# A two-layer encoder trunk on one core: attention outputs from halves, neighbourhood scores over 40 of 64 grid columns, squares on ScalarE, roots put off

## The chip, the cores and the metric

The kernel runs on one core of one Trainium2 chip. The metric is device time in microseconds. Five engines work side by side, each through its own instructions in order: TensorE (PE; its weight loads are listed apart, as PEld), VectorE (DVE), ScalarE (ACT), GpSimd (POOL) and SyncE (SP), which issues all the DMAs here. A change of time within about 0.2% can't be told from none.

## What is computed

Two layers over 256 tokens of 2048 features, float32. Each layer modulates its norms by six vectors made from `c`, runs two attentions side by side with a sigmoid gate each, and then a gated MLP with a convolution over three positions.

```python
for l in range(DEPTH):
    mod = c_act @ ada_w[l] + ada_b[l]
    h = rmsnorm(x, norm_mix[l]) * (1.0 + sc_a) + sh_a
    qa, ka, va, qb, kb, vb, ga, gb = split_cols(h @ w_in[l])
    # A: 8 heads, 2 groups of k and v, q and k normed by head, partial rotary
    ya = window_attention(qa, ka, va, sink_a[l]) @ w_proj_a[l]
    # B: 8 heads, q and k normed by head; tokens lie on a grid of 4 rows of 64 columns
    yb = neighbourhood_attention(qb, kb, vb, rel_bias_b[l]) @ w_proj_b[l]
    merged = jax.nn.sigmoid(ga) * ya + jax.nn.sigmoid(gb) * yb
    x = x + gt_a * (merged @ w_out[l])
    h = rmsnorm(x, norm_ffn[l]) * (1.0 + sc_m) + sh_m
    u = depthwise_conv(h @ w_up[l], conv_w[l], conv_b[l])
    g, v = jnp.split(u, 2, axis=-1)
    x = x + gt_m * ((jax.nn.silu(g) * v) @ w_down[l])
```

In attention A a token sees all tokens up to 128 away. In B it sees all four grid rows, but of each only the 16 columns of a window around its own column, held inside the grid: tokens of columns 0 to 31 see none beyond column 39, and those of 32 to 63 none before 24.

## The kernel before

**The weight stream.** All weights pass once, in units of 16 blocks of 128 x 128 (1 MB). `unit` (L246) loads a unit by one DMA into `raw` (four buffers, shared with the rows `aw` of the modulation weights), and splits each half of it into `hl` (four buffers): the high half is a cast to float32r on ACT (L260), the low half the difference, on DVE (L261). A product of float32 accuracy is then three float32r matmuls: high by high, high by low, low by high (L269 to L271 for a feature block, 256 columns each; L327 to L329 for a token block, 512 columns).

**Ticks.** After each unit `Stream.tick` calls `bg.tick()` and `plan`. `bg` holds deferred functions, called at the next tick, and jobs with a rate, steps per tick. `plan` pulls rows of the modulation (`aw`, L191 and L192, a DMA of 1 MB and a DVE instruction over 2048 elements) by a table of units, ADA_PLAN. So program order is set by ticks; within it the framework's scheduler orders each engine's instructions.

**One layer.** Nine groups of q, k and v columns (in layer 0 four passes over parts of the 16 chunks, with partial sums added into `packs` at L762; in layer 1 one pass, straight out of PSUM), gate A, proj_a over the eight outputs `oA` of attention A, gate B, the merge over `oB`, the output projection, and the MLP. After a group of q or k, `qk_rows` (L487) squares it (L494), sums by head (L495), takes the power −0.5 on POOL (L389), and defers `norm` (L500: DVE multiplies, rotary), which defers `turn` (L523: PE transposes `qtp`, ACT writes q or k transposed with its gain). `turn` then counts the group as ready.

**Attention** is a job: heads are launched once their group is ready, one a step, and each live head goes on by one step: bias load (B only), then `attend` (L535): scores `sc` on PE in float32, masked maximum on DVE (L543), exponential with its sum on ACT (L551), scaling (L559); then transposes `tp` (L564) and a copy (L566); then the product `po` with v in float32 (L570), and its halves (L572, L573). Rates are ATT (1.288 steps a tick in layer 0, 0.4 in layer 1) and, from gate B on, ATT_B (0.21). Before proj_a, `attended(HA)` steps the job until all A heads are done; `bg.finish(job)` before the merge does the rest.

**Bare.** At a layer's start and in the MLP's first chunks, matmuls run on x before the norm's scale is known (class `Bare`, L428): a bare chunk has 256 columns and two more for the shift, a high and a low part in each of its two halves, and `level` (L479) scales the result afterwards. All three matmuls of a block have 258 columns there.

Of the kernel before, what the change touches and what calls it, by code (L numbers as in the profile page):

```python
# [15 lines left out]
P = 128  # L16
# [13 lines left out]
GRID_W, NA_KH, NA_KW = 64, 8, 16  # L30

# [32 lines left out]
ATT = [1.288, 0.4]  # L64
ATT_B = [0.21, 0.21]
# [50 lines left out]
def encoder(ctx: ExitStack, tc: tile.TileContext, a: dict, out: bass.AP):  # L116
# [33 lines left out]
    one = sm.tile([1, P], F32, name="one", tag="one", bufs=1)  # L150
    nc.vector.memset(one[:], 1.0)
    for i in range(0, D, 512):
        cb = ax.tile([P, 512], F32, name="cb", tag="ax")
        nc.tensor.matmul(cb[:], one[:], cact[:1, i : i + 512], start=True, stop=True)
# [3 lines left out]
    skip(224)  # L158
# [106 lines left out]
    def feature_block(ps, hl, j, act, first, last):  # L265

        hi, lo = hl[:, 0, j * P : (j + 1) * P], hl[:, 1, j * P : (j + 1) * P]
        out = ps[:, : act.shape[-1]]
        nc.tensor.matmul(out, hi, act[:, 0], start=first, stop=False)  # L269
        nc.tensor.matmul(out, hi, act[:, 1], start=False, stop=False)  # L270
        nc.tensor.matmul(out, lo, act[:, 0], start=False, stop=last)  # L271
# [72 lines left out]

    def half_tanh(dst, src, **kw):

        nc.scalar.activation(out=dst, in_=src, func=AF.Tanh, scale=0.5, **kw)
# [12 lines left out]
    class Squares:  # L360
# [6 lines left out]
        def add(self, mo):  # L367
            sq = self.acc if mo == 0 else ev.tile([P, S], F32, name="sq", tag="r")
# [59 lines left out]
    class Bare:  # L428
# [23 lines left out]
        def add(self, kc):  # L452
            need(self.l, 48 * self.w + 2 * kc + 2)
            c, scale = self.chunks[kc], amods[self.l][:, self.w, kc : kc + 1]
            sh = mods[self.l][:, 3 * self.w * KC + kc : 3 * self.w * KC + kc + 1]
            nc.scalar.activation(out=c[:, 0, :S], in_=x[:, kc], func=AF.Identity, scale=scale)
            nc.vector.scalar_tensor_tensor(
                out=c[:, 1, :S], in0=x[:, kc], scalar=scale, in1=c[:, 0, :S].bitcast(F32), op0=ALU.mult, op1=ALU.subtract
            )
            sh = sh.broadcast_to([P, 2])  # L460
            nc.scalar.copy(c[:, 0, S:], sh)
            nc.vector.tensor_tensor(out=c[:, 1, S:], in0=sh, in1=c[:, 0, S:].bitcast(F32), op=ALU.subtract)
# [24 lines left out]
    def qk_rows(pss, heads, rot, gain, dst, then):  # L487

        cols = 0
        n = heads * HEAD  # L490
        ss = sm.tile([P, 8], F32, name="qss", tag="qss")
        for t, ps in enumerate(pss):
            sq = at.tile([P, 512], F32, name="qsq", tag="qsq", bufs=1)
            nc.scalar.activation(out=sq[:, :n], in_=ps[:, cols : cols + n], func=AF.Square)  # L494
            nc.vector.tensor_reduce(  # L495
                out=ss[:, t * heads : (t + 1) * heads], in_=sq[:, :n].rearrange("p (h d) -> p h d", d=HEAD), axis=AX.X, op=ALU.add
            )
        rs = sm.tile([P, 8], F32, name="qrs", tag="qrs")
        rsqrt(rs[:, : 2 * heads], ss[:, : 2 * heads], HEAD, 2 * heads)
        def norm():  # L500
            qn = at.tile([P, 2, 4, HEAD], F32, name="qn", tag="qn", bufs=1)
            for t, ps in enumerate(pss):
                nc.vector.tensor_tensor(  # L503
                    out=qn[:, t, :heads],
                    in0=ps[:, cols : cols + n].rearrange("p (h d) -> p h d", d=HEAD),
                    in1=rs[:, t * heads : (t + 1) * heads].unsqueeze(2).broadcast_to([P, heads, HEAD]),
                    op=ALU.mult,
                )
# [14 lines left out]
        def turn(qn):  # L523
            for t in range(2):
                ps = ax.tile([P, 4, P], F32, name="qtp", tag="ax")
                for h in range(heads):
                    nc.tensor.transpose(ps[:, h], qn[:, t, h], ident[:])
                nc.scalar.activation(
                    out=dst[:, :, t * P : (t + 1) * P], in_=ps[:, :heads], func=AF.Identity, scale=gain
                )  # L530
            then()

        bg.defer(norm)

    def attend(qT, kT, v, mask, scale, sink, o):  # L535

        sc = ax.tile([P, 2, S], F32, name="sc", tag="ax")
        for t in range(2):
            nc.tensor.matmul(sc[:, t], qT[:, t * P : (t + 1) * P], kT, start=True, stop=True)  # L539
        p = at.tile([P, 2, S], F32, name="p", tag="p")  # L540
        m = sm.tile([P, 2], F32, name="m", tag="m")
        for t in range(2):
            nc.vector.tensor_tensor_reduce(  # L543
                out=p[:, t], in0=sc[:, t], in1=mask[:, t], scale=scale, scalar=-3.0e38 if sink is None else sink,
                op0=ALU.add, op1=ALU.max, accum_out=m[:, t : t + 1],
            )
# [3 lines left out]
        for t in range(2):  # L550
            nc.scalar.activation(out=p[:, t], in_=p[:, t], func=AF.Exp, bias=nm[:, t : t + 1], accum_out=den[:, t : t + 1])  # L551
# [6 lines left out]
        for t in range(2):  # L558
            nc.scalar.activation(out=p[:, t], in_=p[:, t], func=AF.Copy, scale=ri[:, t : t + 1])  # L559
# [5 lines left out]
        pT = at.tile([P, 2, S], F32, name="pT", tag="pT", bufs=1)  # L565
        nc.scalar.copy(pT[:], tp[:])  # L566
        yield
        po = ax.tile([P, 512], F32, name="po", tag="ax")
        for k in range(2):
            nc.tensor.matmul(po[:, :S], v(k), pT[:, k], start=k == 0, stop=k == 1)  # L570
        o = o()
        nc.scalar.copy(o[:, 0], po[:, :S])  # L572
        nc.vector.tensor_tensor(out=o[:, 1], in0=po[:, :S], in1=o[:, 0].bitcast(F32), op=ALU.subtract)  # L573
# [60 lines left out]
    def small(l):  # L634
# [5 lines left out]
        rg = load(a["rg"][l], [P, 2, ROT], f"rg{l}", lay, tag="rg")  # L640
# [4 lines left out]
        for w in range(2):  # L645
            rot = lay.tile([P, 4, 2, HALF], F32, name=f"rot{l}_{w}", tag=f"rot{w}")
# [9 lines left out]
    for l in range(L):  # L656
# [31 lines left out]
        def va(k, g):  # L688
            return packs[0][:, 2 * k + 1, g * HEAD : (g + 1) * HEAD]
# [4 lines left out]
        def head_a(i):  # L694
# [3 lines left out]
            elif i % 2 == 0:  # L698
# [4 lines left out]
                qTa[:, i], kTa[:, g], lambda k: va(k, g), tables[0], SCALE, sink[:, i : i + 1], lambda: oA[i],  # L703
            )

        def head_b(hb):
# [3 lines left out]
            nc.sync.dma_start(bias[:], a["bias"][l, hb])  # L710
            yield
            yield from attend(
                b[:, 8 + i], b[:, i], lambda k: v[:, k, i * HEAD : (i + 1) * HEAD], bias, 1.0, None,
                lambda: oB_of(hb),
# [31 lines left out]
        for pi, part in enumerate(parts):  # L746
# [4 lines left out]
            for g in range(len(QKV_GROUPS)):  # L751
# [26 lines left out]
                elif vcol is None:  # L778
                    qk_rows(pss, 4, None, gains[:, 3:4] if g in (3, 6) else gains[:, 2:3], dst, have)
# [21 lines left out]
        attended(HA)  # L801
        for mo in range(KC):
# [219 lines left out]
```

## Time and profile before

| | before |
|---|---|
| median of 3 runs | 2705.58 us |
| lowest and highest | 2704.58, 2707.64 us |
| span of the profiled execution | 2703.4 us |
| scores, mean of a record | 382 ns (A), 380 ns (B) |
| output products, mean of a record | 386 ns (A), 391 ns (B) |
| bare matmuls, mean | 284 to 288 ns |
| stream matmuls of 256 columns, mean | 277 to 278 ns |

The profile is of an execution of its own; its span is what all places in time refer to, from 0 to 2703.4. A float32 matmul leaves two records. Matmuls are pipelined, so a record is longer than the step from one start to the next; the steps are read off the timeline. In a group's row stand busy time, mean of one, idle time of the engine before it, and what ended that.

### The profile page before, as it was taken

Reading aid. Unit: us, or ns where it says so; the run is one execution under the profiler, and the core shown is the slowest. Engines: PE = TensorE matmul, PEld = TensorE weight load, DVE = VectorE, ACT = ScalarE, POOL = GpSimd, SP = SyncE. Lnnn points to the kernel's source line nnn. Section 1 sums busy time; section 2 is a strip of 40 time slices with the busy share of each in tenths; the row PEclk is TensorE's granted clock in tenths of the full one; section 3 lists DMA queues with packets and bytes.
Section 4 is the critical chain, followed back from the end, with each engine's and each line's share of the span. In section 5 each row is a group of like instructions: output and inputs, shape, how many; then the busy total and the mean of one; then the engine's idle time right before and its main releaser. Section 6 shows DMA issues by size and latency. Waiting matters only on the chain.

```text
span 2703.4 us, 50143 instructions
## 1 busy us (share of the span) xinstructions
PE 2661.1 (98%) x21088; PEld 2566.7 (95%) x21088; DVE 2099.6 (78%) x2941; ACT 1375.9 (51%) x2026; POOL 34.2 (1%) x24
## 2 busy tenths in 40 slices
PE   7899999999999999999999999999999999999999
PEld 5788799999999999999998889999999999999999
DVE  6998988897988888788886666658879866665664
ACT  5344674455753555355554555544565445544553
POOL 0000100000000000000000000000000000000000
PEclk9999999999999999999999999999999999999999
DMA  8887578986678877887756656666757775555554
GB/s 319 335 335 269 218 282 333 355 316 257 224 291 320 298 272 281 315 295 278 294 211 253 243 203 238 226 244 249 293 183 284 284 257 201 188 197 193 189 199 144
DMA packets 101892, 700.38 MB, mean 259 GB/s; under 512 B 12705, under 2 KB 15009, under 8 KB 17697
## 3 DMA queue, kind: packets, MB, share of 16 engines
q1 hardware_dynamic: 101666, 697.17, 70.3%
q8 instruction: 165, 2.70, 0.4%
q14 instruction: 61, 0.50, 0.0%
HBM read 695.03 MB, written 2.10 MB: 258 GB/s over the span
## 4 chain that ended last, share of the span: by engine, by line
PE 88%; DVE 6%; DMA 2%; issue 2%; ACT 1%; POOL 1%; SPq 0%; DVEq 0%; POOLq 0%; ACTq 0%
PE ps L269 24%; PE ps L271 24%; PE ps L270 24%; PE ps_t L328 4%; PE ps_t L329 4%; PE ps_t L327 4%; DMA aw<-in_aw 2%; DVE hl L261 2%; DVE aw L192 2%; PE po L570 1%; PE sc L539 1%; POOL qrs L389 1%; PE tp L564 0%; ACT hl L260 0%; DVE qn L503 0%
## 5 line engine op out<-in xcount | busy, mean ns | idle before, releaser
L261 DVE TENSOR_TENSOR hl<-w,hl 128x1024 fp32r<-128x1024 f32 x928 | 1129.7, 1223 | 342.1 <-ACT hl L260 341.1
L260 ACT CAST hl<-w 128x1024 fp32r<-128x1024 f32 x928 | 970.6, 1049 | 786.4 <-PE ps L271 497.1
L269 PE MATMUL ps<-h,hl 128*128 128x256 f32 x3328 | 925.7, 278 | 0.0
L271 PE MATMUL ps<-h,hl 128*128 128x256 f32 x3328 | 923.1, 277 | 0.0
L270 PE MATMUL ps<-h,hl 128*128 128x256 f32 x3328 | 922.6, 277 | 0.0
L269 PEld LDWEIGHTS ps<-h,hl 128*128 128x128 f32 x3328 | 625.9, 188 | 0.6
L270 PEld LDWEIGHTS ps<-h,hl 128*128 128x128 f32 x3328 | 625.3, 188 | 0.6
L271 PEld LDWEIGHTS ps<-h,hl 128*128 128x128 f32 x3328 | 625.4, 188 | 0.2
L192 DVE CUSTOM_DVE_ANT_0 aw<-aw,cact,ab 128x2048 f32<-128x2048 f32 x192 | 450.8, 2348 | 73.3 <-DMA aw<-in_aw 72.8
L327 PE MATMUL ps_t<-hl,h 128*128 128x512 f32 x576 | 226.4, 398 | 8.0 <-ACT hl L260 7.3
L328 PE MATMUL ps_t<-hl,h 128*128 128x512 f32 x576 | 227.4, 395 | 5.2 <-DVE hl L261 5.2
L329 PE MATMUL ps_t<-hl,h 128*128 128x512 f32 x576 | 227.0, 394 | 0.9 <-DVE h L418 0.9
L867 DVE SCALAR_TENSOR_TENSOR u<-ps,cw,u 128x255 f32<-128x255 f32 x304 | 146.4, 481 | 89.0 <-ACT u L865 84.5
L865 ACT ACTIVATE u<-ps,cw 128x256 f32<-128x256 f32 x152 | 85.6, 563 | 202.5 <-PE ps L271 202.5
L271 PE MATMUL ps<-merged,hl 128*128 128x256 f32 x512 | 142.1, 278 | 0.4 <-DVE hl L261 0.4
L270 PE MATMUL ps<-merged,hl 128*128 128x256 f32 x512 | 141.7, 277 | 0.0
L269 PE MATMUL ps<-merged,hl 128*128 128x256 f32 x512 | 141.7, 277 | 0.0
L271 PE MATMUL ps<-act_o,hl 128*128 128x256 f32 x512 | 141.5, 276 | 0.0
L270 PE MATMUL ps<-act_o,hl 128*128 128x256 f32 x512 | 141.5, 276 | 0.0
L269 PE MATMUL ps<-act_o,hl 128*128 128x256 f32 x512 | 141.2, 276 | 0.0
L327 PEld LDWEIGHTS ps_t<-hl,h 128*128 128x128 f32 x576 | 109.1, 190 | 31.8 <-ACT hl L260 8.4
L328 PEld LDWEIGHTS ps_t<-hl,h 128*128 128x128 f32 x576 | 109.0, 189 | 30.6 <-DVE hl L261 8.2
(205 smaller groups left out, 4543.2 us busy)
## 6 DMA issues: line engine op xcount, KB each, us to landing
w<-in_ws SPq DMA_DIRECT2D x464, 1024.0 KB, 4.9
aw<-in_aw SPq DMA_DIRECT2D x192, 1024.0 KB, 4.9
bias<-in_bias SPq DMA_DIRECT2D x16, 256.0 KB, 5.0
x<-in_xT SPq DMA_DIRECT2D x4, 512.0 KB, 5.4
out<-x SPq DMA_DIRECT2D x16, 128.0 KB, 2.0
cw<-in_cw SPq DMA_DIRECT2D x2, 176.0 KB, 3.3
maskA<-in_maskA SPq DMA_DIRECT2D x1, 256.0 KB, 5.3
ab<-in_ab SPq DMA_DIRECT2D x2, 48.0 KB, 6.3
```

What stands on the lines that cost most here:

```text
L192: nc.vector.tensor_tensor_reduce(out=raw[:], in0=raw[:], in1=cact[:], scale=1.0, scalar=ab[:, i : i + 1], op0=ALU.mult, op1=ALU.add, accum ...
L260: nc.scalar.copy(hl[:, 0], r)
L261: nc.vector.tensor_tensor(out=hl[:, 1], in0=r, in1=hl[:, 0].bitcast(F32), op=ALU.subtract)
L269: nc.tensor.matmul(out, hi, act[:, 0], start=first, stop=False)
L270: nc.tensor.matmul(out, hi, act[:, 1], start=False, stop=False)
L271: nc.tensor.matmul(out, lo, act[:, 0], start=False, stop=last)
L327: nc.tensor.matmul(ps[:], xh, hi, start=kc == kcs[0], stop=False)
L328: nc.tensor.matmul(ps[:], xh, lo, start=False, stop=False)
L329: nc.tensor.matmul(ps[:], xl, hi, start=False, stop=kc == kcs[-1])
L389: nc.gpsimd.tensor_tensor(out=dst, in0=src, in1=mhalf[:, :k], op=ALU.pow)
L865: nc.scalar.activation(out=u, in_=ps, func=AF.Identity, scale=w[:, 1:2], bias=w[:, 3:4])
L867: nc.vector.scalar_tensor_tensor(out=u[:, to], in0=ps[:, of], scalar=w[:, j : j + 1], in1=u[:, to], op0=ALU.mult, op1=ALU.add)
```

## The change

**Outputs from halves.** `attend` splits the transposed weights `p` into halves (ACT cast, DVE difference, 512 wide), `halves_of` splits v (once a group in A, once a head in B), and `po` becomes six float32r matmuls instead of two float32 ones.

**B's scores over 40 columns.** `turn` writes B's q in the order (column half, grid row, column), so that the first 128 queries are the left half of the grid and the last the right. Each set is multiplied with 40 of the 64 columns of k: 160 score columns instead of 256. The maximum, exponential and scaling run over these; the 96 others of `p` are set to zero on POOL. The bias is loaded in the new order of queries, in four DMAs a head; the outputs are written back in token order.

**Squares.** Each head's square is an ACT instruction with an accumulated sum, in place of a wide square on ACT and a sum on DVE.

**Roots put off.** `norm` is deferred by PUT_OFF = 3 ticks more.

**Bare.** A chunk's first half holds the shift's high and low part in its two more columns; the matmul with the second half has 256 columns, and `level` adds the two columns with an accumulated copy.

**Pace and buffers.** From `attended(HA)` to gate B the job's rate is ATT_A (0.5 in layer 0, 0.4 in layer 1). Some small pools lose a buffer.

```diff
+GRID_R, COLS, SEEN = S // GRID_W, GRID_W // 2, 40
+PUT_OFF = 3
 ATT = [1.288, 0.4]
+ATT_A = [0.5, 0.4]
...
         nc.tensor.matmul(out, hi, act[:, 0], start=first, stop=False)
-        nc.tensor.matmul(out, hi, act[:, 1], start=False, stop=False)
+        nc.tensor.matmul(ps[:, :S], hi, act[:, 1, :S], start=False, stop=False)
         nc.tensor.matmul(out, lo, act[:, 0], start=False, stop=last)
...
+    def split_of(dst, src):
+
+        nc.scalar.copy(dst[:, 0], src)
+        nc.vector.tensor_tensor(out=dst[:, 1], in0=src, in1=dst[:, 0].bitcast(F32), op=ALU.subtract)
...
-            nc.scalar.activation(out=sh[:], in_=ps[:, S : S + 1], func=AF.Copy, scale=scale)
+            parts = sm.tile([P, 2], F32, name="lpt", tag="lpt")
+            nc.scalar.activation(out=parts[:], in_=ps[:, S : S + 2], func=AF.Copy, scale=scale, accum_out=sh[:])
...
+    def put_off(n, fn):
+
+        bg.defer((lambda: put_off(n - 1, fn)) if n else fn)
...
-            sq = at.tile([P, 512], F32, name="qsq", tag="qsq", bufs=1)
-            nc.scalar.activation(out=sq[:, :n], in_=ps[:, cols : cols + n], func=AF.Square)
-            nc.vector.tensor_reduce(
-                out=ss[:, t * heads : (t + 1) * heads], in_=sq[:, :n].rearrange("p (h d) -> p h d", d=HEAD), axis=AX.X, op=ALU.add
-            )
+            for h in range(heads):
+                sq = ev.tile([P, S], F32, name="qsq", tag="r", bufs=2)
+                nc.scalar.activation(
+                    out=sq[:, :HEAD], in_=ps[:, h * HEAD : (h + 1) * HEAD], func=AF.Square, accum_out=ss[:, t * heads + h : t * heads + h + 1]
+                )
...
-        bg.defer(norm)
+        put_off(PUT_OFF, norm)
+
+    def halves_of(v):
+
+        hl = at.tile([P, ROW - OFF + 4 * HEAD], F32R, name="vh", tag="vh")
+        hl = hl[:, ROW - OFF :].rearrange("p (a k d) -> p a k d", a=2, k=2)
+        split_of(hl, v)
+        return hl[:, 0], hl[:, 1]
...
+        if grid:
+            for t in range(2):
+                first = (1 - t) * SEEN
+                hidden = p[:, t].rearrange("p (r c) -> p r c", r=GRID_R)[:, :, first : first + GRID_W - SEEN]
+                nc.gpsimd.memset(hidden, 0.0)
         for t in range(2):
-            nc.tensor.matmul(sc[:, t], qT[:, t * P : (t + 1) * P], kT, start=True, stop=True)
+            nc.tensor.matmul(sc[:, t, :n], qT[:, t * P : (t + 1) * P], seen(t, kT), start=True, stop=True)
...
-        pT = at.tile([P, 2, S], F32, name="pT", tag="pT", bufs=1)
-        nc.scalar.copy(pT[:], tp[:])
+        pT = at.tile([P, 2, 2, S], F32R, name="pT", tag="pT", bufs=1)
+        split_of(pT, tp[:])
+        vh, vl = v()
         yield
         po = ax.tile([P, 512], F32, name="po", tag="ax")
         for k in range(2):
-            nc.tensor.matmul(po[:, :S], v(k), pT[:, k], start=k == 0, stop=k == 1)
+            for i, (w, a) in enumerate(((vh, 0), (vh, 1), (vl, 0))):
+                nc.tensor.matmul(po[:, :S], w[:, k], pT[:, a, k], start=k == 0 and i == 0, stop=k == 1 and i == 2)
...
-            nc.sync.dma_start(bias[:], a["bias"][l, hb])
+            for r in range(GRID_R):
+                rows = a["bias"][l, hb].rearrange("(r i c) t s -> r t c i s", r=GRID_R // 2, i=2)
+                nc.sync.dma_start(bias[r * COLS : (r + 1) * COLS], rows[r % 2, r // 2])
...
         attended(HA)
+        bg.pace(job, ATT_A[l])
```

**The order on PE in units 52 and 53 of layer 0**, the first of proj_a. Names: `ps` is an output block of proj_a, `oA` an A head's output (4 holds heads 4 and 5; 6 and 7 their own), `hl` split weights. Before, B's heads 3 and 4 stand between runs of proj_a, and head A7 is long there:

```order
L271 MATMUL ps_52_16_0_3350<-oA_7_2730,hl_52_0_3353 128x256
L269 MATMUL ps_53_8_0_3384<-oA_0_2276,hl_52_1_3356 128x256
L564 MATMUL tp<-ident,p 128x128
L539 MATMUL sc<-packB_1_189 128x256
L564 MATMUL tp<-ident,p 128x128 x3
L539 MATMUL sc<-packB_1_189 128x256
L270 MATMUL ps_53_8_0_3384<-oA_0_2276,hl_52_1_3356 128x256
```

Now heads A6 and A7 are transposed in these units; four blocks of proj_a are open at once, and each waits for `oA_7`:

```order
L272 MATMUL ps_54_8_0_3494<-oA_6_2968,hl_53_1_3466 128x256
L273 MATMUL ps_54_8_0_3494<-oA_6_2968,hl_53_1_3466 128x256
L610 MATMUL tp<-ident,p 128x128
L584 MATMUL sc<-packB_0_183 128x160 x2
L610 MATMUL tp<-ident,p 128x128 x3
L539 MATMUL qtp<-ident,qn 128x128 x8
L618 MATMUL po<-pT,vh 128x256 x6
L271 MATMUL ps_52_16_0_3353<-oA_7_3070,hl_52_0_3356 128x256
```

What moved: A7's transposes and product stand in proj_a, with no block of gate A left between them.

**The order on DVE at that place**, of the changed kernel, from a row of the modulation (L194) through A6's split (the first L350) and A7's maxima (L587) to A6's output:

```order
L194 ISA aw_45_3685,mod_139<-aw_45_3685,cact,ab_140 128x2048
L194 ISA mod_139 128x1
L350 TENSOR_TENSOR pT<-tp,pT 128x512
L587 ISA p,m<-sc,maskA,sink_215 128x256
L587 ISA m 128x1
L587 ISA p,m<-sc,maskA,sink_215 128x256
L587 ISA m 128x1
L592 TENSOR_SCALAR nm<-m 128x2
L626 TENSOR_TENSOR oA_6_2968<-po,oA_6_2968 128x256
```

What moved: before, A's maxima had casts of weights and rows of gate A between them; now a 2048-wide row of the modulation stands ahead of the split and the maxima, and another ahead of A7's split.

**The order on ACT where group 1's squares stand in layer 0** (`packA` holds the group's sums, `hl` weights ahead of use). Before:

```order
L494 ACTIVATE qsq<-packA_187 128x512
L260 CAST hl_40_1_2220<-w_40_2215 128x1024
L494 ACTIVATE qsq<-packA_187 128x512
L528 ACTIVATE packA_187<-qtp,gains_216 128x2x128 x2
L260 CAST hl_41_0_2282<-w_41_2280 128x1024
```

Now:

```order
L507 ACTIVATE qsq,qss<-packA_182 128x128 x8
L262 CAST hl_40_1_2184<-w_40_2179 128x1024
L262 CAST hl_41_0_2251<-w_41_2249 128x1024
L507 ACTIVATE qsq,qss<-packA_182 128x128 x8
L262 CAST hl_41_1_2254<-w_41_2249 128x1024
```

What moved: eight short squares stand in one piece ahead of the cast that stood between two long ones, and the write of the transposed keys is further behind.

More of the change, by code (lines that the diff above doesn't have):

```diff
@@ L157, in encoder @@
     skip(96, const)
-    skip(224)
     sp = pool("s", 1)
@@ L527, in turn @@
                     nc.tensor.transpose(ps[:, h], qn[:, t, h], ident[:])
[L528 to L537 removed]
+                if not grid:
+                    nc.scalar.activation(
+                        out=dst[:, :, t * P : (t + 1) * P], in_=ps[:, :heads], func=AF.Identity, scale=gain
+                    )
+                    continue
@@ new lines, in turn @@
+                for i in range(2):
+                    at = i * P + t * 2 * COLS
+                    nc.scalar.activation(
+                        out=dst[:, :, at : at + 2 * COLS].rearrange("p h (r c) -> p h r c", r=2),
+                        in_=ps[:, :heads].rearrange("p h (r i c) -> p h i r c", r=2, i=2)[:, :, i],
+                        func=AF.Identity, scale=gain,
+                    )
+            then()
+        put_off(PUT_OFF, norm)
[4 more added lines that the diff above has]
+        return hl[:, 0], hl[:, 1]
```

69 lines of the change are left out of this document (44 added, 25 removed).

## The prediction

> **What bounds the kernel now.** I read the page's first part, then the table of stretches, then PE's own waits, then single matmuls in the timeline.
>
> ```profile
> PE 2661.1 (98%) x21088; PEld 2566.7 (95%) x21088; DVE 2099.6 (78%) x2941; ACT 1375.9 (51%) x2026; POOL 34.2 (1%) x24
> PE 88%; DVE 6%; DMA 2%; issue 2%; ACT 1%; POOL 1%; SPq 0%; DVEq 0%; POOLq 0%; ACTq 0%
> 260.00:280.00 20.00, 16.02 (x81) 13.00 (x80) 17.31 (x35) 11.32 (x17) 5.31 (x2) 1.00 0.43 158
> 280.00:300.00 20.00, 17.92 (x84) 14.18 (x83) 18.36 (x32) 11.88 (x22) 1.64 (x1) 1.00 0.69 262
> 300.00:320.00 20.00, 18.92 (x91) 15.03 (x90) 18.15 (x40) 14.58 (x33) 5.24 (x2) 1.00 0.56 211
> 320.00:340.00 20.00, 20.00 (x133) 18.03 (x132) 18.31 (x38) 14.60 (x33) 2.59 (x1) 1.00 0.57 212
> 340.00:360.00 20.00, 19.21 (x149) 18.25 (x148) 19.95 (x42) 16.30 (x39) 0.00 (x0) 1.00 0.81 294
> 360.00:380.00 20.00, 19.79 (x141) 18.19 (x141) 16.91 (x43) 14.76 (x36) 0.00 (x0) 1.00 0.90 336
> 380.00:400.00 20.00, 19.51 (x142) 18.06 (x141) 15.82 (x37) 12.35 (x28) 0.00 (x0) 1.00 0.68 252
> 400.00:420.00 20.00, 19.36 (x162) 18.87 (x161) 16.65 (x25) 8.98 (x14) 0.00 (x0) 1.00 0.82 304
> 1500.00:1600.00 100.00, 100.00 (x463) 83.23 (x463) 67.58 (x106) 56.74 (x90) 4.91 (x3) 1.00 0.62 227
> 2300.00:2400.00 100.00, 100.00 (x881) 100.00 (x881) 67.72 (x92) 53.25 (x74) 0.00 (x0) 1.00 0.55 193
> ```
>
> Columns of a stretch: its length, then busy time of PE, PEld, DVE, ACT, POOL, then clock, DMA share, GB/s. From 420 on PE is full, layer 1's attention (1500 to 1600) included: there a column less on PE is time off the end. The exception is layer 0's attention, 260 to 420. PE is idle there for 160 − 150.7 = 9.3 us, and DVE is busy 141.5 of 160, 19.95 of 20 at its worst: two engines near their limit.
>
> **The change: PE's sum.** A head's output products and a B head's scores, then 20 consecutive matmuls of 256 columns (first and last), then 34 of the bare ones with 258:
>
> ```profile
> 1670.11 0.86 PE po L570 x4
> 1671.41 0.86 PE sc L539 x4
> ...
> 1171.76 0.28 PE L269 MATMUL ps<-h,hl 128*128 128x256 f32 x1
> 1173.91 0.28 PE L270 MATMUL ps<-h,hl 128*128 128x256 f32 x1
> ...
> 700.17 0.28 PE L269 MATMUL ps<-bare_b,hl 128*128 128x258 f32 x1
> 704.15 0.28 PE L269 MATMUL ps<-bare_qn,hl 128*128 128x258 f32 x1
> ```
>
> - **Outputs.** Two f32 products are four records in 0.86 us. Six products of halves have the shape of the stream's, (1173.91 − 1171.76)/19 = 0.113 us apart: 0.68. So 0.18 us a head, over 32 heads **−5.8**.
> - **B's scores.** Four records of 256 columns in 0.86; at 160, if time goes with columns, 0.54: 0.32 a head, over 16 heads **−5.2**. The operand becomes rows of 40 out of 64, a pattern the trace doesn't show, so the other end is 0 (a loss beyond that I exclude: no more columns than before). I take the full value, nearest the row.
> - **Bare.** 512 of 1536 bare matmuls go from 258 to 256. Start to start a bare one takes (704.15 − 700.17)/33 = 0.1206, 7.4 ns over the 0.1132 of a 256. If the two columns cost all of that, 512 × 7.4 ns = 3.8; if only their share of the columns, 2/258 × 0.1206 = 0.9 ns, 0.5. Bare and normal operands lie in different tiles, so the gap may not be width alone; I take the middle, **−2.2**.
>
> The Trainium skill (TensorE: Matmul & The Clock Gate, section Back-to-back issue gap) gives a stream of warm matmuls as N/2.4 + 2.5 ns, 109.2 for 256 and 110.0 for 258. By that rule the narrowing is worth 0.4 us in all; the trace's 113.2 and 120.6 are further apart than the rule has them, and nothing here separates width from placement.
>
> PE's sum is −13.2 of which layer 0, with half the heads, holds 5.5.
>
> **Off PE.** The costs are group means (line, engine, operation, shapes, count; busy us, mean ns; idle before); the last row is ACT's wait, over the whole run, for PE to give back a buffer of split weights:
>
> ```profile
> L495 DVE TENSOR_REDUCE qss<-qsq 128x4 f32<-128x512 f32 x12 | 8.2, 680 | 0.0
> L762 DVE TENSOR_TENSOR packB<-ps_t,packB 128x512 f32<-128x512 f32 x12 | 8.1, 682 | 0.2 <-PE ps_t L329 0.2
> L192 DVE CUSTOM_DVE_ANT_0 aw<-aw,cact,ab 128x2048 f32<-128x2048 f32 x17 | 39.9, 2345 | 1.7 <-DMA aw<-in_aw 1.7
> L543 DVE CUSTOM_DVE_ANT_0 p<-sc,maskA,sink 128x256 f32<-128x256 f32 x16 | 7.1, 482 | 0.4 <-PE sc L539 0.4
> L573 DVE TENSOR_TENSOR oA<-po,oA 128x256 fp32r<-128x256 f32 x8 | 3.3, 418 | 0.4 <-ACT oA L572 0.4
> ...
> L494 ACT ACTIVATE qsq<-ps_t 128x512 f32<-128x512 f32 x12 | 7.1, 592 | 4.1 <-PE ps_t L329 4.0
> L551 ACT ACTIVATE p<-p,nm 128x256 f32<-128x256 f32 x64 | 32.0, 501 | 26.5 <-DVE nm L548 26.5
> L551 ACT ACTIVATION_READ_ACCUMULATOR p<-p,nm 128x1 f32 x64 | 12.0, 187 | 0.0
> ...
> ACT hl L260 <- PE ps L271: 497.1, 373, 4.3
> ```
>
> - **Squares.** A four-head group loses two reductions (1.36 us of DVE) and two squares of 512 (1.18 of ACT), and gains eight of 128 with an accumulator read. A square of 128 lies between 0.15 (a quarter of 592) and 0.50 (the 256-wide exponential); with 0.19 for the read, 2.7 to 5.5 us of ACT, say 3.8. ACT is at most 16.3 of 20 busy in the stretch, and its casts run until PE has no free buffer for them (497 us of such waits), so this lead hides it; uncovered, it costs 3.8 − 1.18 = 2.6 us for each of twelve groups.
> - **Halves.** A head adds one DVE subtraction of 512 (0.68, by L762's row) and a B head one of 256 (0.42) and its cast on ACT; A's are made once a group of four heads. DVE in layer 0: −8.2 for reductions, +16 × 0.68, +10 × 0.42, a little off for narrower scores: about +6. But the lower pace moves some three B heads out of this stretch to after 420, where PE covers them. DVE in the stretch stays near 140 us.
> - **Memsets of hidden cells** run on POOL, 1% busy, before the scores; **bias rows** in four DMAs each instead of one: three more issues a head on SP's queue, ahead of the next weights. Both are hidden by the units of lead. At worst one landing of 5 us per head is late in the places below.
> - **Narrow shift in `level`**: one accumulator read more, 32 × 0.19 us of ACT behind a full PE: nothing.
> - **Roots put off by three ticks.** Who waited for whom (us in total, times, longest): PE's waits in 260 to 420, DVE's there for POOL's powers, and PE's only one in layer 1's attention:
>
> ```profile
> PE qtp L527 <- DVE qss L388: 2.7, 1, 2.7
> PE qtp L527 <- DVE qn L503: 1.8, 1, 1.8
> PE qtp L527 <- DVE qn L520: 1.3, 1, 1.3
> ...
> DVE qn L503 <- POOL qrs L389: 6.9, 6, 1.5
> ...
> PE qtp L527 <- DVE qn L520: 1.4, 1, 1.4
> ```
>
> The transposes (qtp) make PE idle 2.7 + 1.8 + 1.3 = 5.8 us. With the normalisation three ticks later the power is long done: **−5.8**, and DVE gets up to 6.9 us back. In layer 1 the PSUM pair of a group is held longer, but DVE normalises it two units before PE needs the buffer.
>
> **What is late next.** The put-off delays the A heads by three units of about 5.4 us (48 × 0.113), yet proj_a needs all eight: `attended(HA)` now forces the last three, A5 to A7, and two B heads follow at once. Before, PE ran gates between them. Now, between A7's scores and its transposes PE has only A6's output (0.68) and 12 products (1.36). The chain there: the rest of an aw (about 0.9), A6's split 0.68, two masked maxima 1.1, negation 0.16, two exponentials 1.4, the sink's 0.3, sum and reciprocal 0.3, the first scaling 0.5: 5.3 us, so 3.3 idle. After A7's transposes another aw (2.4), B0's maxima and A7's split stand before the output: 4.7 against 1.9 of work, 2.8 idle; then its halves, 0.8; then DVE must split unit 54's weights behind B1's work, 1 to 2. Sum **+8.5**, bounds +3 (aw arrives early) to +20 (below). Elsewhere in the stretch idle of 3.5 us (9.3 − 5.8) stays.
>
> Sum: −13.2 − 5.8 + 8.5 = −10.5; with the 1.4 of layer 1's one wait of the same kind, **−12**. Against this profile's span of 2703.4 that is 2691.4. The median of the runs is 2705.58, 2.2 above the span, so I predict **2693.5**.
>
> **Rivals.**
> 1. *The forced heads cost more than they free (slower).* Place: units 52 to 54 of layer 0. If A5, A6, A7, B0 and B1 each stand exposed for the 5.3 us chain plus an aw of 2.4, less 2 of work, that is 5 × 5.7 = 28 us: −13.2 − 5.8 + 28 = +9, 2715. At 19 us of idle it has eaten the gain, at 24 it shows. For it: DVE has aw rows inside these chains. Against: 72 products fill the first two.
> 2. *The clock falls there.* At 72 to 79 PE stood still for 7 us, and its clock then was halved:
>
> ```profile
> 75.00:80.00 5.00, 0.82 (x2) 0.50 (x2) 4.93 (x7) 2.38 (x3) 0.00 (x0) 0.50 0.96 347
> 80.00:85.00 5.00, 3.95 (x11) 2.86 (x11) 5.00 (x6) 1.70 (x3) 0.00 (x0) 0.55 1.00 378
> 79.17 1.22 PE L327 MATMUL ps_t<-hl,h 128*128 128x512 f32 x2 [7.04 <-ACT hl L260]
> ```
>
> The loss after it is 5 × 0.50 + 5 × 0.45 = 4.8 us of clock. Waits of 2.7 us left it at 1.00 (260 to 280). With one such fall: 2698. The Trainium skill (TensorE: Matmul & The Clock Gate, section What's actually happening) says that an idle window of about 3.4 us halves the clock; the 3.3 us above is right beside it, and the trace agrees on both sides, 2.7 and 7.0.
> 3. *Widths pay little.* Scores keep their time and bare gains 0.5: 2693.5 + 5.2 + 1.7 = 2700.4, no change by the measure below.
> 4. *The stretch heals.* PE's idle of 9.3 vanishes and the forced heads cost 3 only: −13.2 − 9.3 + 3 = −19.5, 2686; with bare at its full 3.8, 2684.
>
> **Numbers.** Own case 0.50 (2688 to 2697), healing 0.19, the clock 0.14, narrow widths 0.11, slower 0.06. The range takes the bounds of bare (±1.7), the forced heads and the clock: **2683 to 2700**. A measurement of this kernel can tell about 0.2%, 5.4 us, from no change. Faster by more (below 2700.2) are my case, the healing, most of the clock's and some of the narrow widths': 0.84. The rest of these two and the mildest of the first rival are the same: 0.11. Slower: 0.05.
>
> **What would show it.** Per head po 0.68 and B's scores 0.54 in the chain of waits (scores near 0.86 would refute the strided operand); bare starts 0.113 to 0.118 apart on one line in three; no PE wait at qtp on DVE; idle PE at the po and tp of A6 to B0, 6 to 10 us in all, and clock 1.00 there; from 420 on PE full as before. I'm wrong if new idle appears in layer 1 (a held PSUM pair, late bias), or if the masks on POOL make the scores wait.

## The result, and the profile after

| kernel | median us | runs | lowest to highest | ratio to before, 95% |
|---|---|---|---|---|
| before | 2706.61 | 4 | 2704.58 to 2710.49 | 1 |
| changed | 2685.79 | 4 | 2683.23 to 2687.83 | 0.9921 (0.9907 to 0.9935) |

The changed kernel is 20.8 us, 0.8%, faster. Its profiled execution has a span of 2683.2 us (2685.71 as a run), 20.2 below the span of before. Forecast were 2693.5 in 2683 to 2700 and a gain of 12. The sign and the range held; the size is that of the fourth rival, the healing stretch (2686), though not by that rival's terms, as the last part shows.

First the page of the changed kernel, its first part and its chain that ended last; then the stretches of layer 0's attention, with the columns of the prediction's table:

```profile
PE 2647.0 (99%) x21152; PEld 2559.6 (95%) x21152; DVE 2101.2 (78%) x2964; ACT 1393.7 (52%) x2266; POOL 36.3 (1%) x56
PE 92%; DVE 3%; DMA 2%; issue 1%; ACT 1%; POOL 0%; DVEq 0%; ACTq 0%
```

```profile
260.00:280.00 20.00, 20.00 (x92) 16.56 (x91) 19.31 (x32) 14.39 (x53) 7.33 (x3) 1.00 0.87 347
280.00:300.00 20.00, 19.52 (x98) 16.07 (x98) 20.00 (x37) 14.25 (x44) 4.89 (x2) 1.00 0.67 242
300.00:320.00 20.00, 20.00 (x129) 17.85 (x128) 19.85 (x37) 16.05 (x43) 1.70 (x2) 1.00 0.77 292
320.00:340.00 20.00, 19.97 (x166) 19.22 (x165) 19.27 (x44) 17.17 (x41) 0.00 (x0) 1.00 0.70 261
340.00:360.00 20.00, 19.92 (x158) 18.96 (x158) 18.84 (x42) 12.56 (x33) 0.00 (x0) 1.00 0.69 242
360.00:380.00 20.00, 15.39 (x95) 12.83 (x94) 13.38 (x36) 13.47 (x35) 0.89 (x6) 0.91 0.48 166
380.00:400.00 20.00, 20.00 (x173) 19.91 (x172) 19.57 (x36) 12.60 (x27) 0.89 (x6) 1.00 0.82 290
400.00:420.00 20.00, 20.00 (x176) 20.00 (x175) 17.12 (x35) 10.32 (x21) 0.30 (x2) 1.00 0.71 258
```

The idle of PE from 260 to 360 went from 7.93 us to 0.59, although DVE is busier than before: 18.84 to 20.00 of 20 in these five stretches, where it was 17.31 to 19.95, and 147.3 us in 260 to 420 where it was 141.5. From 360 to 380 stands a new hole of 4.6 us (the expectations below call it the drain). Busy time hides part of this: a matmul counts as busy for its whole 0.28 us, while a full PE starts one each 0.1135. I therefore also summed every start-to-start step of a matmul less its usual one (0.1135 us for 256 columns, 0.2265 for 512, 0.120 for a bare product, layer 1's undisturbed steps for scores and outputs). That "loss", worked out from the trace and good to about 1 us because it depends on the usual steps chosen, is 19.2 us before and 15.4 after in 260 to 420: 2.0 and 9.4 of it in 360 to 380, 17.3 and 6.0 in the other seven stretches.

PE's own waits in 260 to 420 (who waited for whom: us, times, longest) show the same. Of the three waits of before at qtp on DVE nothing is left; the largest is the outputs' wait for the low half of the probabilities, in the hole:

```profile
PE po L618 <- DVE pT L350: 2.0, 3, 1.4
PE ps L271 <- ACT oA L625: 0.9, 2, 0.5
PE ps L273 <- DVE hl L263: 0.6, 1, 0.6
PE tp L610 <- ACT p L605: 0.5, 1, 0.5
PE qtp L539 <- ACT qsq L507: 0.5, 1, 0.5
```

The timeline of PE in layer 1, where nothing stalls it, prices the narrower products. First before, then the changed kernel:

```profile
1669.95 1.02 PE L570 MATMUL po<-pT,packA 128*128 128x256 f32 x4
1670.81 0.60 PE L564 MATMUL tp<-ident,p 128*128 128x128 f32 x4
1671.25 1.03 PE L539 MATMUL sc<-packB 128*128 128x256 f32 x4
1671.92 0.47 PE L269 MATMUL ps<-h,hl 128*128 128x256 f32 x1
```

```profile
1666.32 0.87 PE L618 MATMUL po<-pT,vh 128*128 128x256 f32 x6
1667.03 0.60 PE L610 MATMUL tp<-ident,p 128*128 128x128 f32 x4
1667.46 0.71 PE L584 MATMUL sc<-packB 128*128 128x160 f32 x4
1667.90 0.39 PE L271 MATMUL ps<-h,hl 128*128 128x256 f32 x1
```

From start to the next one's start an output takes 0.71 us instead of 0.86, a B score 0.44 instead of 0.67. The whole of layer 1 agrees: 0.153 and 0.24 us less a head.

### The profile page after: what moved, and what is told of

It reads as the page before. It is cut to its first block, busy times and chain, and to the rows that moved or that the text cites. A ratio compares the mean times of both kernels' runs of the same rounds, so it can differ in the third digit from the quotient of the medians.

```text
span 2683.2 us, 50732 instructions
## 1 busy us (share of the span) xinstructions
PE 2647.0 (99%) x21152; PEld 2559.6 (95%) x21152; DVE 2101.2 (78%) x2964; ACT 1393.7 (52%) x2266; POOL 36.3 (1%) x56
## 4 chain that ended last, share of the span: by engine, by line
PE 92%; DVE 3%; DMA 2%; issue 1%; ACT 1%; POOL 0%; DVEq 0%; ACTq 0%
PE ps L271 25%; PE ps L273 25%; PE ps L272 25%; PE ps_t L330 5%; PE ps_t L331 5%; PE ps_t L329 5%; DMA aw<-in_aw 2%; DVE aw L194 1%; DVE hl L263 1%; PE sc L584 1%; PE po L618 1%; PE tp L610 1%; PE qtp L539 0%; PE cb L157 0%; ACT hl L262 0%
## 5 line engine op out<-in xcount | busy, mean ns | idle before, releaser
L194 DVE CUSTOM_DVE_ANT_0 aw<-aw,cact,ab 128x2048 f32<-128x2048 f32 x192 | 450.9, 2349 | 81.5 <-DMA aw<-in_aw 81.1
L273 PE MATMUL ps<-act_o,hl 128*128 128x256 f32 x512 | 141.5, 276 | 0.0
L272 PE MATMUL ps<-act_o,hl 128*128 128x256 f32 x512 | 141.5, 276 | 0.0
```

Of the source, the lines that this page charges most:

```text
L194: nc.vector.tensor_tensor_reduce(out=raw[:], in0=raw[:], in1=cact[:], scale=1.0, scalar=ab[:, i : i + 1], op0=ALU.mult, op1=ALU.add, accum ...
L272: nc.tensor.matmul(ps[:, :S], hi, act[:, 1, :S], start=False, stop=False)
```

## The experiments

Theory P: the put-off emptied layer 0's stretch. Theory S: taking the squares off DVE did. Two further questions were the hole at 360 to 380, and whether the bare term is width. All differ from the changed kernel as shown; the changed kernel itself ran twice, at 2685.79 and (beside the last group) 2684.04. Before, measured again beside each of the three groups, had 2705.29, 2704.31 and 2704.35, so a difference of 1 us between groups says nothing.

| run | median us (runs) | ratio to before, 95% | loss in 260 to 420 | of it 360 to 380 |
|---|---|---|---|---|
| no_putoff | 2688.53 (4) | 0.9925 to 0.9955 | 17.1 | 1.6 |
| dve_squares | 2694.36 (9) | 0.9953 to 0.9973 | 17.0 | 3.9 |
| no_pace | 2688.12 (4) | 0.9923 to 0.9953 | 17.1 | 9.1 |
| bare_wide | 2721.43 (4) | 1.0047 to 1.0077 | 16.4 | 9.3 |
| bare_wide_same_place | 2691.98 (5) | 0.9939 to 0.9969 | 13.9 | 8.3 |
| bare_264 | 2688.81 (4) | 0.993 to 0.9959 | 15.1 | 9.0 |
| put_off_1 | 2682.66 (4) | 0.9905 to 0.9935 | 11.6 | 2.1 |
| put_off_2 | 2683.36 (4) | 0.9912 to 0.9941 | 11.6 | 3.5 |
| changed_again | 2684.04 (5) | 0.9915 to 0.9943 | 13.8 | 8.3 |
| f32_out | 2705.37 (11) | 0.9993 to 1.0011 | 8.6 | 1.7 |
| full_scores | 2693.50 (5) | 0.9952 to 0.9977 | 14.7 | 7.1 |
| roots_squares_back | 2700.51 (11) | 0.9977 to 0.9995 | 25.3 | 0.9 |

### Roots and squares, each and both undone

```diff
-PUT_OFF = 3
+PUT_OFF = 0
```

> The changed kernel with the roots used one tick after the squares, as before (PUT_OFF 0). Theory P (the put-off is what emptied layer 0's stretch of waits): PE's waits at qtp come back, 6 to 9 us of idle in 260 to 360, while the drain at 360 to 380 (4.6 us idle and 1.8 of clock) shrinks, so the time moves by less than 3 us either way, 2683 to 2689. Theory S (the squares taken off DVE emptied it): qtp waits stay below 1.5 us and only the drain shrinks: 3 to 6 us faster, 2680 to 2683.

```diff
-            for h in range(heads):
+            for h in range(0, heads, 2):
                 sq = ev.tile([P, S], F32, name="qsq", tag="r", bufs=2)
-                nc.scalar.activation(
-                    out=sq[:, :HEAD], in_=ps[:, h * HEAD : (h + 1) * HEAD], func=AF.Square, accum_out=ss[:, t * heads + h : t * heads + h + 1]
+                nc.scalar.activation(out=sq[:], in_=ps[:, h * HEAD : (h + 2) * HEAD], func=AF.Square)
+                nc.vector.tensor_reduce(
+                    out=ss[:, t * heads + h : t * heads + h + 2], in_=sq[:].rearrange("p (h d) -> p h d", d=HEAD), axis=AX.X, op=ALU.add
                 )
```

> The changed kernel with q and k's squares summed by a DVE reduction again (256-wide squares on ScalarE, 24 reductions of 2x128 in layer 0's and 24 in layer 1's groups, some 0.4 us each). Theory P: the roots have three ticks of slack, so some 9 us more of DVE per layer stay hidden: within 2 us, 2684 to 2688. Theory S: DVE, at 19.3 to 20.0 of 20 busy in 260 to 340, has no room, and 6 to 9 us of PE idle come back: 2692 to 2695.

The third kernel of this group has both edits at once.

> The changed kernel with both the put-off undone (PUT_OFF 0) and the squares summed on DVE again; PE's products stay as changed. If the two are independent, their losses add: 2.7 + 8.6, 2697. If the squares only hurt because the put-off and the forced heads leave DVE no room (theory C, the stretch is one budget of DVE), the drain is gone and the stretch looks as before the change (16 us of loss in 260 to 420, qtp waits of 4 to 6 us): 2688 to 2692.

PE's waits in 260 to 420 of no_putoff, then in 280 to 470 of dve_squares, then in 260 to 420 of roots_squares_back:

```profile
PE qtp L539 <- DVE qn L532: 2.3, 1, 2.3
PE tp L610 <- ACT p L605: 1.6, 1, 1.6
PE qtp L539 <- DVE qn L515: 1.3, 1, 1.3
```

```profile
PE ps L271 <- ACT hl L262: 3.8, 3, 1.8
PE ps_t L330 <- DVE hl L263: 2.1, 1, 2.1
PE ps L273 <- DVE hl L263: 1.1, 2, 0.8
PE qtp L540 <- DVE qn L533: 0.9, 1, 0.9
```

```profile
PE qtp L540 <- DVE qn L533: 3.4, 2, 2.2
PE qtp L540 <- DVE qn L516: 2.2, 1, 2.2
PE ps_t L330 <- DVE hl L263: 1.8, 2, 1.1
PE ps L273 <- DVE hl L263: 1.7, 2, 1.5
PE ps L271 <- DVE packB L822: 1.5, 1, 1.5
PE po L619 <- DVE pT L350: 1.1, 1, 1.1
```

Without the put-off the qtp waits are back, 3.6 us, as theory P has it, and the hole at 360 to 380 is gone, so the time moves by only 2.7 to 4.5 us. Its profile is 5.9 us longer than that of the changed kernel: 1.7 of this lie in 260 to 420, and 4.0 in 560 to 1400 (6.3 of loss against 2.3), where PE waits 3.1 us for DVE's halves of weights. Whether that part belongs to the put-off stays open.

But dve_squares is 8.6 to 10.3 us slower, which P had ruled out: now the casts and the splits of weights are late. In 260 to 420 it loses little more than the changed kernel, 17.0 against 15.4, for its hole is smaller; in the other seven stretches it loses 13.1 against 6.0, and by the same reckoning about 6 us more in 420 to 560 and 4 more in 560 to 1400. Its reductions are a little dearer than those of before (26 of 0.41 us a layer, 10.8, where before had 12 of 0.68 and 2 of 0.41, 9.0). So neither theory stands alone.

With both undone the kernel loses 14.7 to 16.5 us, more than 2.7 + 8.6 or 4.5 + 10.3 by 3.4 and 1.7, which is no more than runs of one kernel spread. Theory C's 2688 to 2692 is refuted: the hole went, as it said, but the stretch is worse than before the change, 25.3 us of loss against 19.2; the halves, which are still there, are the likely reason (f32_out below). What PE waits for, in all three, is for the greater part DVE (normalised heads, halves of weights, sums), and in dve_squares ACT's casts of weights beside it. Shorter products on PE alone, without either relief of DVE, bring 3.8 us (2704.35 to 2700.51 in that group) of the 11 that their steps save.

### The hole: forced heads

```diff
-PUT_OFF = 3
+PUT_OFF = 1
```

> The changed kernel with the roots put off by one tick instead of three. Theory: one tick (16 blocks, 5.4 us of products) outlasts the power's wait of 1.5 us, so the qtp waits of 2.4 and 1.5 us that came back without the put-off stay away, and the A heads start two ticks earlier, so the drain at 360 to 380 loses 4 to 8 of its 9 us: 2678 to 2683. Rival (DVE's queue, not the power, makes qtp late): qtp waits of 2 us or more are back and the time is that of no_putoff, 2686 to 2690.

> The changed kernel with the roots put off by two ticks. By the same theory the qtp waits stay away and the drain loses 2 to 6 us: 2680 to 2685. Rival as for one tick.

```diff
-        bg.pace(job, ATT_A[l])
```

> The changed kernel without the lower rate of attention after the A heads (1.288 steps a tick in layer 0 as before, not 0.5). Theory R (the lower rate keeps B heads from crowding DVE right after the forced drain): 3 to 6 more us of PE idle in 370 to 420, 2689 to 2692. Rival: the drain is set by the forced A heads alone, and the heads after it hide behind the gates: within 1 us of the changed kernel.

The stretch 360 to 380 of put_off_1, then of changed_again, which is the changed kernel a second time:

```profile
360.00:380.00 20.00, 19.81 (x160) 18.83 (x160) 18.91 (x42) 14.66 (x35) 0.89 (x6) 1.00 0.78 272
```

```profile
360.00:380.00 20.00, 15.47 (x104) 12.64 (x103) 14.79 (x38) 14.24 (x36) 1.19 (x8) 1.00 0.47 157
```

> The changed kernel itself once more, for its spread beside the three others of this call: 2683 to 2688, and in the profile the same 9 us of loss at 360 to 380 if that loss belongs to the order of instructions and not to chance.

The times of put_off_1, put_off_2 and changed_again fall into their ranges. One tick keeps the qtp waits away (0.7 us is left of them in 260 to 420) and empties the hole; two ticks leave 3.5 us of loss in it. So the hole belongs to the three ticks of delay, and it repeats in the second profile. That `attended(HA)` turns the delay into a hole is read from the order of instructions; no run here takes it out. Put_off_1 is 1.4 to 3.1 us below the changed kernel: its interval, 0.9905 to 0.9935, overlaps the changed kernel's, so it isn't shown to be faster; nor do three ticks show any gain over one. The 6 us that its stretch gains over changed_again at 360 to 380 are partly given back at 380 to 420 (3.9 against 0.8) and 560 to 1400 (3.8 against 1.3). The lower rate of attention is worth 2 to 4 us by the medians and 2 us by the loss at 380 to 420: it leaves the hole as it is, and that is less than the 3 to 6 its theory wanted and more than the rival's 1. The intervals of no_pace and of the changed kernel overlap, so the median alone doesn't show it.

### The bare products, and what an address costs

```diff
-        nc.tensor.matmul(ps[:, :S], hi, act[:, 1, :S], start=False, stop=False)
+        nc.tensor.matmul(out, hi, act[:, 1], start=False, stop=False)
...
-            parts = sm.tile([P, 2], F32, name="lpt", tag="lpt")
-            nc.scalar.activation(out=parts[:], in_=ps[:, S : S + 2], func=AF.Copy, scale=scale, accum_out=sh[:])
+            nc.scalar.activation(out=sh[:], in_=ps[:, S : S + 1], func=AF.Copy, scale=scale)
```

> The changed kernel with all three bare products 258 columns wide and the shift split in two columns of both halves, as before. Theory W0 (a bare start step is set by something other than 256 against 258 columns, since all of them run at 0.119 to 0.120): within 0.7 us of the changed kernel. Rival, the prediction's term: 2.2 us slower (0.5 to 3.8), with steps of 0.113 to 0.118 gone from one bare line in three.

It is 35 us above the changed kernel, nine times the rival's most. The time wasn't in the bare products. The timeline of PE at products that the edit doesn't touch, first and last of 33 in a row, of the changed kernel, then of bare_wide:

```profile
1092.73 0.28 PE L271 MATMUL ps<-act_b,hl 128*128 128x256 f32 x1
1096.36 0.28 PE L273 MATMUL ps<-act_b,hl 128*128 128x256 f32 x1
```

```profile
1103.10 0.28 PE L271 MATMUL ps<-act_b,hl 128*128 128x256 f32 x1
1106.94 0.28 PE L273 MATMUL ps<-act_b,hl 128*128 128x256 f32 x1
```

3.63/32 is 0.1134 us a step, 3.84/32 is 0.1200. The edit took away a tile of two columns, and with it every tile allocated behind it moved. The next kernel is the same with that tile kept, and one more short ACT copy for each output block of a bare product, so that the tile and its neighbour stay in use.

> As bare_wide (all three bare products 258 wide, shift in both halves), but with the small tile of the changed kernel's level kept, so that every operand keeps the SBUF address of the changed kernel: all float32r operands start 32 bytes past a multiple of 64. In bare_wide that tile was gone, 5527 of the 256-wide products had both successive activations at a multiple of 64, and started 0.120 apart instead of 0.1135 on the mean: 5527 x 6.4 ns = 35 us, all that it lost. Theory A (address, not width): 0.113 steps are back everywhere outside bare, and the time is within 1 us of the changed kernel's 2685.8. Rival W (width of the middle product): 2 to 4 us slower than the changed kernel. Rival N (the 35 us had another cause than address): again near 2721.

Its profiled span is 2683.2, the changed kernel's to 0.1 us, and the 0.120 steps outside bare are gone. Theory N is refuted: most or all of the 35 us came with the addresses (35.7 between the two profiles, 29 between the medians). For the width, first and last of 24 bare products, in the changed kernel and in this one:

```profile
691.22 0.28 PE L271 MATMUL ps<-bare_b,hl 128*128 128x258 f32 x1
693.95 0.28 PE L273 MATMUL ps<-bare_b,hl 128*128 128x258 f32 x1
```

```profile
694.99 0.28 PE L271 MATMUL ps<-bare_b,hl 128*128 128x258 f32 x1
697.77 0.28 PE L273 MATMUL ps<-bare_b,hl 128*128 128x258 f32 x1
```

2.73/23 is 0.1187, 2.78/23 is 0.1209: narrowing one product of three makes the three about 2 ns quicker on the mean. The mean over all of them is 120.4 against 122.0 ns, 2.5 us for 1536. Its five runs spread from 2685.12 to 2695.86, so that the median, 6 to 8 us above the changed kernel, meets neither theory; the steps speak for W's size, and the rest of the median stays unexplained.

```diff
-                    self.chunks.append(c[:, :, : S + 2])
+                    self.chunks.append(c[:, :, : 264])
```

> The changed kernel with 264 columns instead of 258 in the two wide bare products (the six more repeat the shift's low half and are read by nobody), so that a row ends on a multiple of 32 bytes as a 256-wide one does. Theory E (258 columns end inside a 32-byte piece, and that sets 0.120): bare steps fall to 0.113 to 0.117, 5 to 10 us faster, 2676 to 2681. Rival: steps follow the columns, 0.120 plus 6 x 0.42 ns on 1024 products, 2.6 us slower.

Rows of 264 are no way out: their steps are 123.7 ns on the mean, the 256-wide ones between them 118.0, and the time is 3.0 to 4.8 us above the changed kernel. Theory E is refuted.

### The outputs and the scores by themselves

```diff
-        pT = at.tile([P, 2, 2, S], F32R, name="pT", tag="pT", bufs=1)
-        split_of(pT, tp[:])
-        vh, vl = v()
+        pT = at.tile([P, 2, S], F32, name="pT", tag="pT", bufs=1)
+        nc.scalar.copy(pT[:], tp[:])
+        vk = v()
...
-            for i, (w, a) in enumerate(((vh, 0), (vh, 1), (vl, 0))):
-                nc.tensor.matmul(po[:, :S], w[:, k], pT[:, a, k], start=k == 0 and i == 0, stop=k == 1 and i == 2)
+            nc.tensor.matmul(po[:, :S], vk[:, k], pT[:, k], start=k == 0, stop=k == 1)
```

> The changed kernel with the outputs of both attentions as one float32 product again (no halves of the probabilities and of v). The prediction's term: 32 heads x (0.86 - 0.71 us) = 4.8 slower; against it, DVE loses a 512-wide subtraction of 0.68 us per head and PE's waits for it in the drain (1.42 + 0.34 us): net 2 to 5 slower, 2688 to 2691. Rival H (the halves' work on DVE and ScalarE costs layer 0 as much as PE gains): no slower than the changed kernel, 2683 to 2687.

20 us slower than the changed kernel, four to ten times the expected loss. Most of this goes with an address again: the smaller tiles moved those behind them. 33 of the same products, from the timeline of f32_out:

```profile
1094.56 0.28 PE L271 MATMUL ps<-act_b,hl 128*128 128x256 f32 x1
1098.33 0.28 PE L273 MATMUL ps<-act_b,hl 128*128 128x256 f32 x1
```

3.77/32 is 0.1178. 5508 products there have this step, 117.8 on the mean against 113.8: 22 us (24 against the 113.6 that the same kinds of product take in the changed kernel). Taking 22 off its span of 2703.7 leaves 2681.7, and 24 leaves about 2680; the two profiles of the changed kernel have 2683.2 and 2679.7. So the halves on the whole seem to bring nothing here (rival H), but that is worked out, not run: a version of f32_out with every address kept was not tried. What a slower step can't explain is a wait that goes. The stretch 360 to 380 of f32_out:

```profile
360.00:380.00 20.00, 20.00 (x153) 19.03 (x152) 14.07 (x39) 15.69 (x40) 0.89 (x6) 1.00 0.60 210
```

The hole is gone though the roots are put off by the same three ticks: with one copy between the transposes and the output, and no subtraction on DVE behind an aw of 2.35 us, the chain is short enough, as far as one profile shows. The halves save 0.153 us of PE on 32 heads, 4.9, and cost 5 to 7 us in layer 0's stretch (13.8 to 15.4 against 8.6).

```diff
-dst, have, grid=g in (5, 8))
+dst, have)
...
-            for r in range(GRID_R):
-                rows = a["bias"][l, hb].rearrange("(r i c) t s -> r t c i s", r=GRID_R // 2, i=2)
-                nc.sync.dma_start(bias[r * COLS : (r + 1) * COLS], rows[r % 2, r // 2])
+            nc.sync.dma_start(bias[:], a["bias"][l, hb])
...
-                lambda: oB_of(hb), grid=True,
+                lambda: oB_of(hb),
```

> The changed kernel with B's scores over all 64 grid columns again (256 wide, one bias transfer a head, no memsets, queries not regrouped). The prediction's term: 16 heads x (0.86 - 0.54) = 5.1 slower, plus wider maxima and exponentials on DVE and ScalarE that layer 0 may feel by 0 to 3: 2691 to 2694. Rival: less than 2 slower, if the narrow form's four transfers, memsets and strided reads cost about what the columns save.

7.7 to 9.5 us slower, 2693.5 where 2691 to 2694 was expected: 16 x 0.24 = 3.9 on PE, and the rest is loss that is spread over the kernel (0 to 260, 420 to 1400; in 260 to 420 it is 14.7 where the changed kernel has 15.4 and 13.8), not collected at layer 0's heads. Which of these is the wider masks and maxima on DVE and which is chance, one profile can't say.

## Why the prediction was right or wrong

The sum from profile to profile, forecast and found, in us (the gain is 20.2):

| term | forecast | found |
|---|---|---|
| outputs, 32 heads | −5.8 | −4.9 (0.153 each) |
| B's scores, 16 heads | −5.2 | −3.9 (0.24 each) |
| bare products | −2.2 | −2.5 |
| layer 0's stretch without 360 to 380 | −5.8 | −11.3 |
| 360 to 380, the forced heads | +8.5 | +7.4 |
| layer 1's attention, 1480 to 1880 | −1.4 | −4.0 |
| everywhere else | 0 | −1.0 |

- **The products** went as described. They were priced too high by 2.2, since the quoted 0.86 of a score was the duration of four records, with the end of the last one in it; 0.67 to the next start was the step to use. The output's six steps came at 0.118, not 0.113. That the bare third runs at about 0.120 and not at 0.113 to 0.118 refutes the mark that I gave for it, while the middle value of its price was right: the gain falls on all three. As the middle of two bounds with no mechanism behind it, that was luck. The section of the Trainium skill that the prediction names (TensorE: Matmul & The Clock Gate, section Back-to-back issue gap) calls its formula the gap of isolated matmuls, and gives other figures for a stream with weight loads. Here rows of 258 came at 122.0 ns on the mean and 256 columns at 113.8.
- **The step that failed** is the sentence "Elsewhere in the stretch idle of 3.5 us (9.3 − 5.8) stays", with the squares costed at nothing. I looked at ACT's room for the squares and found it hidden, rightly: a square of 128 takes 0.298 us and its read 0.187, eight of them 3.88 where 3.8 was said. I didn't price what it takes off DVE, since DVE's sum came out even ("near 140 us"; it came to 147.3, and PE waited less all the same). Undone alone it costs 9 to 10 us, and with the put-off undone too 15 to 16. The 7 us of loss that dve_squares puts back in the seven stretches (13.1 against 6.0) are near the 5.5 that the forecast lacks there, though the run shows it by what comes back, and not by a chain that was followed through. And idle by the busy column was too small a measure: the stretch lost 19.2 us by start steps, not 9.3.
- **The put-off** did what the step says: no PE wait at qtp on DVE (2.3 and 1.3 us come back without it), and what is late next is the forced heads, where I put them. Its own balance against PUT_OFF 0 is only 2.7 to 4.5 us, as the hole takes back most.
- **The forced heads** cost 7.4 against 8.5, at the place named, but not by the waits described. PE's waits in the hole add up to 4.6 us: 3.1 at po and tp, where 6 to 10 were to show, and 1.5 at products of proj_a. None is over 1.4, where the sum had 3.3 and 2.8. The rest of the loss went in gaps too short to be listed and in a slower clock (0.91 of 20 us, 1.8), which was to stay at 1.00. That the sizes meet is in part luck.

This is the place in PE's timeline of the changed kernel, each row with the wait before it; an aw of 2.35 us stands on DVE from 367.64:

```profile
362.75 0.85 PE L618 MATMUL po<-pT,vh 128*128 128x256 f32 x5 [0.34 <-DVE pT L350]
366.24 0.33 PE L610 MATMUL tp<-ident,p 128*128 128x128 f32 x1 [0.48 <-ACT p L605]
368.85 0.38 PE L618 MATMUL po<-pT,vh 128*128 128x256 f32 x1 [0.35 <-ACT packB L547]
370.65 0.86 PE L618 MATMUL po<-pT,vh 128*128 128x256 f32 x5 [1.42 <-DVE pT L350]
```

- **Layer 1** gained its one wait, 1.4, and 1.3 more because the 384 products of oB ran at 0.1145 on the mean where before had 0.1178. Before's layer 0 read the same tiles at 0.1133, so that no address explains it, and such a step comes and goes: put_off_2, with every operand at the changed kernel's address, has 0.1175 at these products. I can only say that this part is there, not that the change made it. The last 1.3 of the 4.0 stay open.
- **Rivals.** The slower one has no support. The clock one came about in one profile of two, at 1.8 us by the clock's column instead of 4.8; no_pace, bare_wide and bare_264 show the same 0.91 over the same hole, bare_wide_same_place and full_scores 1.00. Narrow widths are refuted: of the scores' 5.2 a quarter was missing, of bare nothing. The healing stretch is what happened, though not with forced heads at +3: the products brought 1.9 less than its sum has, the stretch 2.0 more, the forced heads cost 4.4 more, and layer 1, which its sum leaves out, brought 4.0. That its 2686 was met is in part luck.

## What to carry to other kernels

Where two engines stand near their limit, price a change on both: the shorter products without the two reliefs of DVE brought 3.8 us, and undoing both reliefs cost 15 to 16, though DVE's busy time was the same before and after (2099.6 and 2101.2 us). Measure idle time by start steps against the step of a full stretch, since busy time counts the tail of each matmul. And when an experiment removes or shrinks a buffer, keep the addresses of all others, or the result may be about the address.

## What the runs showed of the hardware

**Step and address.** The step of a 256-column float32r product went with where in SBUF its activation starts. These are means over the whole trace, sorted by the programs' allocation, with weights that start 32 bytes past a multiple of 256. Activations at 224 past one take 113.8 ns on the mean (15952 steps of the changed kernel; before has them there too, and the diff's removed pad of 224 bytes is part of what keeps them). At 96 they take 117.8 (5508, f32_out), at 128 120.0 (5510, bare_wide), at 32 116.3 (607, changed kernel). With the weights at 224 as well it is 119.9 (113 steps). Only bare_wide against bare_wide_same_place tests it as a cause, 2718.9 against 2683.2 of span; the other places weren't set on purpose, and why they differ stays open. Nor is the address all: layer 1's products of oB took 117.8 in before and 117.5 in put_off_2 with activations at 224.

**The clock and short waits.** The first profile of the changed kernel, where idle pieces add up, falls to half clock (the clock is the third column from the end):

```profile
368.00:370.00 2.00, 0.88 (x5) 0.45 (x4) 2.00 (x3) 1.53 (x5) 0.00 (x0) 1.00 0.34 76
370.00:372.00 2.00, 0.88 (x6) 0.68 (x6) 0.89 (x4) 1.29 (x6) 0.00 (x0) 0.90 0.63 141
372.00:373.00 1.00, 1.00 (x5) 1.00 (x6) 0.71 (x2) 0.87 (x3) 0.00 (x0) 0.50 0.97 401
```

Its second profile kept 1.00 over the same hole (the row of changed_again above). The half clock lasted 3.4 us: 0.4 before 372, and 0.50 in each row up to 375. In no_putoff one wait of 2.27 us was enough, as the rows below show, and in before one of 2.71 was not (its stretch 260 to 280 stands at 1.00 in the prediction):

```profile
268.00:269.00 1.00, 0.00 (x0) 0.00 (x0) 1.00 (x5) 0.04 (x1) 0.00 (x0) 1.00 0.99 131
269.00:270.00 1.00, 0.59 (x6) 0.62 (x7) 1.00 (x4) 1.00 (x7) 0.00 (x0) 1.00 0.64 254
270.00:271.00 1.00, 1.00 (x7) 0.90 (x6) 1.00 (x2) 1.00 (x8) 0.00 (x0) 0.61 0.98 418
```

So the length of a wait alone doesn't decide between 2.3 and 2.7 us. The Trainium skill (TensorE: Matmul & The Clock Gate, section What's actually happening) says that activity is judged in free-running windows of about 3.4 us. That the same hole sometimes meets it and sometimes not, and that the half clock lasted as long (3.4 us), agrees; that one idle window of that length is needed does not.
